# Attention and merge of a hybrid layer without GpSimd, and weight halves kept in DRAM

## The chip, the cores and the metric

The kernel runs on one core of a Trainium2 chip. It is timed as microseconds of device time for one launch; the time before is 2791.53 us, the median of three runs (2789.71 to 2792.70).

## The reference

One layer over 1024 tokens of width 1024 with a 256-token context: a layer norm, a projection, two branches (a bidirectional state-space scan with a gated output, and windowed attention of 8 query heads on 2 key heads with a sink in the softmax), a merge, a second norm and a mixture of experts (top 4 of 32). What the change touches is this part:

```
s_loc = where(|kpos - qpos| <= 128, q k^T, -1e30);  s_ctx = q kc^T
p = softmax([s_loc, s_ctx, sink]);  o_att = p_loc v + p_ctx vc
m = sig(g_ssm) * (z @ w_ssm_out) + sig(g_att) * (o_att @ w_att_out)
mix = m @ w_o
h = LN(alpha * h + gate1 * mix)
ffn = moe(modulate(h, shift2, scale2));  out = LN(alpha * h + gate2 * ffn)
```

All inputs and outputs are float32. The kernel keeps that precision by writing an operand as a rounded high half plus the rest, and by three matmuls (high by high, high by low, low by high) for each product.

## The kernel before

The program has three long parts. The first, up to about 545 us, holds the input norm, the projections and the scan. The second, from about 545 to 1130 us, runs attention, the branch outputs, the merge and the routing, woven into each other; the change lies here. The third, to the end, streams the weights of 32 experts.

In the second part `attention` (from L513) takes 8 blocks of 128 queries, each in two units, one for a key head. In a unit `scores` makes the scores of four query heads, two at a time: matmuls into PSUM, row maxima on DVE (L589 to L594), exponentials with row sums on ACT (L598, L600), the reciprocal of the sum on DVE (L604 to L606), and the normalisation of the probabilities P in place, on GpSimd (L608). `values` then transposes P on TensorE (L621), splits it into halves (ACT makes the high one, DVE the low one, L42 and L43) and multiplies by V.

A `Filler` puts pieces of other work between these steps: `glu` and `ssm_out`, beside which `residual` (L708) rescales the normed input row by row (a multiply and an add on GpSimd, L721 and L722), and then `merge` (L754). `merge` works on groups g of 256 tokens. `branches` needs two column pieces of w_att_out, `mix` four of w_o; each piece is 1 MB. `weights` (L793) keeps two pieces ready: `load_w` (L259) loads a raw piece, ACT writes its high half `whi`, and the low half `wlo` is made by GpSimd or by DVE in turn (`eng` in L795). The buffers `raw`, `whi` and `wlo` have two places each. So the first three groups take six pieces each; the last group takes two of w_att_out and two of w_o, and the two other pieces of w_o lie in buffers of their own, `wo` (L242), that are filled when attention has ended. `norm` (L850) makes the normed rows h and the modulated rows `xm`, whose last add is on GpSimd (L862). `residual2` (L1536) prepares the final sum for each of 8 token tiles: it loads a row block, multiplies it by a constant row on GpSimd (L1552), adds a small matmul on DVE (L1561), and stores it.

The order on each engine is set by a scheduler that places the instructions of the program when it is built, so a change of one engine shifts the order on all. All loads and stores of this part are issued from the one queue of SyncE (SP), in their order; an issue that has to wait holds up all behind it. From the last group's mixing on, the order of DVE, then also of TensorE and ACT, is the order of the code.

Of the kernel before, what the change touches and what calls it, by code (L numbers as in the profile page):

```python
# [8 lines left out]
F32 = mybir.dt.float32  # L9
F32R = mybir.dt.float32r  # L10
# [3 lines left out]
ACTF = mybir.ActivationFunctionType  # L14
ALU = mybir.AluOpType
# [7 lines left out]
KT = 8  # L23
# [5 lines left out]
ALPHA = 2.0 ** 0.25  # L29
# [52 lines left out]
def body(tc, a, o):  # L82
    nc = tc.nc
    K = Ctx()
    es = ExitStack()
    with es:
        cst = es.enter_context(tc.tile_pool(name="cst", bufs=1))
        dram = es.enter_context(tc.tile_pool(name="dram", bufs=1, space=DRAM))
        K.ident = cst.tile([128, 128], F32, name="ident")
        nc.sync.dma_start(out=K.ident, in_=a["ident"])  # L90
        K.cols = cst.tile([128, 68], F32, name="cols")
        nc.sync.dma_start(out=K.cols, in_=a["cols"])
        K.xhat_d = dram.tile([S, D], F32, name="xhat_d")
        K.rows_d = dram.tile([4, D], F32, name="rows_d")
        K.xm_d = dram.tile([S, D], F32, name="xm_d")
        K.acc_d = dram.tile([S + 128, D], F32, name="acc_d")
        K.kv_d = dram.tile([NCTX + S, 256], F32, name="kv_d")
        K.q_d = dram.tile([S, 512], F32, name="q_d")
        K.gate_d = dram.tile([16, 128, S], F32, name="gate_d")
        K.o_d = dram.tile([4, 128, S], F32, name="o_d")  # L100
        K.ssm_d = dram.tile([8, 128, S], F32, name="ssm_d")
        K.z_d = dram.tile([S, 512], F32, name="z_d")
        K.win_d = dram.tile([4, 128, 8 * 2 * 128], F32, name="win_d")
        K.wout_d = dram.tile([4, 128, 2 * 8 * 128], F32, name="wout_d")
        K.m_d = dram.tile([4, 128, 8 * 128], F32, name="m_d")
        K.tab_d = dram.tile([64, 34], F32, name="tab_d")
        K.tabe_d = dram.tile([64, 1], I32, name="tabe_d")
        K.cst = cst
        K.mask = cst.tile([128, 8, 2, 32], BF16, name="mask")
        K.gts = cst.tile([128, 8, 32], F32, name="gts")  # L110
        K.b_cols = a["b_cols"]
        pre(tc, a, K, es)
        moe(tc, a, K)
        finish(tc, a, o, K)
# [28 lines left out]
def pre(tc, a, K, top):  # L143
    nc = tc.nc
    es = ExitStack()
    with es:
# [88 lines left out]
        with ExitStack() as ws:  # L235
            wo = pool(ws, "wo")
            K.rk = pool(ws, "rk")
            rank_consts(tc, a, K, K.rk)
            K.ps = pool(ws, "lps", 2, space=PSUM)
            K.lp = pool(ws, "lgp", 1, space=PSUM)  # L240
            residual2_consts(tc, a, K, pool(ws, "res2"))
            K.wo = [load_w(tc, K, a["w_o"][:, c * 256:(c + 1) * 256], to=[wo.tile([128, KT, 256], F32R, name="wo%d%d" % (c, i)) for i in range(2)])  # L242
                    for c in range(2)]
            while not K.last:
                fl.emit()
            with tc.manual_schedule(engines={mybir.EngineType.DVE}):
                fl.drain()
                for r in K.todo:
                    next(r)
# [263 lines left out]
def attention(tc, a, K, es, fl):  # L513
    nc = tc.nc
# [19 lines left out]
    for g0, n in ((8, 2), (0, 4), (4, 4)):  # L534
        p = K.tp.tile([128, 512], F32, tag="tp", name="tp")
        for i in range(n):
            t = g0 + i
# [28 lines left out]
    def scores(n, kv, pr, Q):  # L566

        b0, b1 = max(0, n - 1), min(8, n + 2)
        nl = (b1 - b0) * 128
# [35 lines left out]
        nc.vector.tensor_tensor(su[:, 0], su[:, 0], su[:, 2], ALU.add)  # L605
        nc.vector.reciprocal(su[:, 0], su[:, 0])  # L606
        for i in range(2):
            nc.gpsimd.tensor_scalar(P[i][:, 0:nl + 256], P[i][:, 0:nl + 256], su[:, 0, i:i + 1], 1.0, ALU.mult, ALU.mult)  # L608
        return P

    def values(n, kv, P):
# [96 lines left out]
def residual(tc, a, K, es):  # L708

    nc = tc.nc  # L710
    pool = es.enter_context(tc.tile_pool(name="res", bufs=2, side="right"))
    for c in range(2):
        cs = slice(c * 512, (c + 1) * 512)
        gb = pool.tile([128, 2, 512], F32, tag="gb", bufs=1, name="gb")
        nc.sync.dma_start(out=gb, in_=a["ln_rows"][2:4, cs].unsqueeze(0).to_broadcast([128, 2, 512]))
        nc.gpsimd.tensor_scalar(gb, gb, ALPHA, 1.0, ALU.mult, ALU.mult)
        for t in range(8):
            x = pool.tile([128, 512], F32, tag="x", name="x")
            d = K.xhat_d[t * 128:(t + 1) * 128, cs]
            nc.sync.dma_start(out=x, in_=d)  # L720
            nc.gpsimd.tensor_tensor(x, x, gb[:, 0], ALU.mult)  # L721
            nc.gpsimd.tensor_tensor(x, x, gb[:, 1], ALU.add)  # L722
            nc.sync.dma_start(out=d, in_=x)
            yield

# [25 lines left out]
    return wn, out[:, 0], out[:, 1]  # L751


def merge(tc, a, K, es):  # L754

    nc = tc.nc
# [14 lines left out]
    def consts():  # L771
        nc.sync.dma_start(out=rb, in_=bc(K.rows_d[0:3], 3))
        v.tensor_scalar(G2, G2, 1.0, None, ALU.add)
        x0 = hp.tile([128, D], F32, tag="xm", name="x0")
        nc.sync.dma_start(out=x0, in_=a["ln_rows"][1:2, :].to_broadcast([128, D]))
        nc.gpsimd.tensor_tensor(x0, x0, G2, ALU.mult)
        nc.gpsimd.tensor_tensor(B2, B2, x0, ALU.add)
        x0 = hp.tile([128, D], F32, tag="xm", name="x0")
        nc.sync.dma_start(out=x0, in_=a["ln_rows"][0:1, :].to_broadcast([128, D]))
        nc.gpsimd.tensor_tensor(G2, G2, x0, ALU.mult)  # L780
        x0 = hp.tile([128, D], F32, tag="xm", name="x0")
        nc.gpsimd.memset(x0, 0.0)
        nc.sync.dma_start(out=K.acc_d[S:S + 128, :], in_=x0)
        nc.sync.dma_start(out=wr, in_=a["w_router"].rearrange("(k p) e -> p k e", p=128))
        nc.sync.dma_start(out=br, in_=a["b_router"].unsqueeze(0).to_broadcast([128, 32]))
        nc.sync.dma_start(out=e32, in_=a["route"][:, 384:416])

    sources = [s for g in range(4) for s in
               [(a["w_att_out"][:, c * 512:(c + 1) * 512], 512, 4) for c in range(2)] +
               [(a["w_o"][:, c * 256:(c + 1) * 256], 256, 8) for c in range(0 if g < 3 else 2, 4)]]  # L790
    ready = []

    def weights():  # L793
        while len(ready) < 2 and sources:
            ready.append(load_w(tc, K, *sources.pop(0), eng=nc.gpsimd if len(sources) % 2 else None))  # L795
        return ready.pop(0)

    def gates(g, c):
# [51 lines left out]
    def norm(g, h):  # L850
# [5 lines left out]
        for i in range(2):  # L856
            t = g * 2 + i
            v.tensor_scalar(h[i], h[i], mv[:, i, 0:1], r[:, i:i + 1], ALU.subtract, ALU.mult)
            nc.sync.dma_start(out=K.xhat_d[t * 128:(t + 1) * 128, :], in_=h[i])
            x = hp.tile([128, D], F32, tag="xm", name="xm")  # L860
            v.tensor_tensor(x, h[i], G2, ALU.mult)
            nc.gpsimd.tensor_tensor(x, x, B2, ALU.add)  # L862
            nc.sync.dma_start(out=K.xm_d[t * 128:(t + 1) * 128, :], in_=x)
            h[i] = x

# [670 lines left out]
def residual2(tc, K, t, h=None, eng=None, q=None):  # L1536
# [8 lines left out]
    for c in range(2):  # L1545
# [3 lines left out]
            nc.sync.dma_start(out=x, in_=K.xhat_d[t * 128:(t + 1) * 128, cs])  # L1549
        else:  # L1550
            x = h[:, cs]
        nc.gpsimd.tensor_tensor(x, x, K.ga[:, cs], ALU.mult)  # L1552
        xs.append(x)
    yield
    for c, x in enumerate(xs):
# [689 lines left out]
```

## Time and profile before

| what | value |
|---|---|
| median of three runs | 2791.53 us |
| the profiled execution | 2796.39 us |
| its span, first to last instruction | 2794.6 us |
| attention, branches, merge, routing | about 545 to 1130 us |
| busy over the span: PE, DVE, ACT, POOL | 90%, 80%, 52%, 17% |

The span is the time between the first and the last instruction of the profiled execution; 1.8 us lie around it. A busy share is an average over parts with different limits: the third part keeps TensorE nearly full, and the part that the change touches does not. PE is TensorE, PEld its weight loads, DVE VectorE, ACT ScalarE, POOL GpSimd, SP the queue that issues transfers.

### The profile page before, as it was taken

To read this page: it belongs to the slowest core of one execution; us is meant where nothing else is said; L and a number is where in the kernel's file an instruction comes from. 1 tells how busy PE (TensorE), PEld (TensorE's weight loads), DVE (VectorE), ACT (ScalarE), POOL (GpSimd) and SP (SyncE) were. 2 spreads that over 40 slices of the span, in tenths; PEclk is the share of its full clock that TensorE was granted. 3 is DMA by queue.
4 is the path that set the end of the run, shared out by engine and by line. 5 is a ranking of instruction groups with operands and counts; after the bars stand their busy time and mean duration, and the time that the engine had idled before them with its cause. 6 is when DMAs were issued, how large, how long until landed. Compare 5 with 4: busy or idle time off the path is not lost. (4 is left out here: it accounts for less than half of the span.)

```text
span 2794.6 us, 41588 instructions
## 1 busy us (share of the span) xinstructions
PE 2523.9 (90%) x14030; PEld 2123.3 (76%) x14030; DVE 2234.2 (80%) x4306; ACT 1465.9 (52%) x2352; POOL 465.0 (17%) x303
## 2 busy tenths in 40 slices
PE   6799999978887877699999999999999999999990
PEld 1698887767686767588888888889888887888770
DVE  9636796347788887788878888888988899899995
ACT  0623113656555422455656666666666666666661
POOL 3200000034333243210110110110111011101113
PEclk8799999979998877699999999999999999999995
DMA  7434623554454463678979978988998999899983
GB/s 252 155 125 157 202 87 116 161 172 136 163 169 139 146 195 102 209 244 266 290 226 284 295 242 283 292 273 272 303 294 262 305 301 300 275 305 302 311 280 144
DMA packets 409674, 631.11 MB, mean 226 GB/s; under 512 B 36497, under 2 KB 215569, under 8 KB 408497
## 3 DMA queue, kind: packets, MB, share of 16 engines
q1 hardware_dynamic: 397152, 584.37, 63.8%
q0 software_dynamic: 11872, 42.47, 6.5%
q8 instruction: 112, 1.84, 0.3%
q10 hardware_dynamic: 432, 1.57, 0.2%
q14 instruction: 106, 0.86, 0.1%
HBM read 551.76 MB, written 76.57 MB: 225 GB/s over the span
## 5 line engine op out<-in xcount | busy, mean ns | idle before, releaser
L1478 DVE TENSOR_TENSOR wl<-raw,wh 128x1024 fp32r<-128x1024 f32 x768 | 920.8, 1219 | 163.4 <-ACT wh L1476 162.3
L1476 ACT ACTIVATE wh<-raw 128x1024 fp32r<-128x1024 f32 x768 | 790.3, 1052 | 246.5 <-PE dn L1294 87.9
L1344 PE MATMUL uw<-x,wh 128*128 128x320 f32 (+5 forms) x1920 | 581.3, 366 | 0.2 <-issue 0.2
L1345 PE MATMUL uw<-x,wl 128*128 128x192 f32 (+4 forms) x1920 | 501.4, 261 | 0.0
L1344 PEld LDWEIGHTS uw<-x,wh 128*128 128x128 f32 x1920 | 364.3, 190 | 24.0 <-issue 0.3
L1345 PEld LDWEIGHTS uw<-x,wl 128*128 128x128 f32 x1920 | 369.6, 193 | 0.5
L1291 PE MATMUL dn<-wh,a 128*128 128x512 f32 (+4 forms) x752 | 298.7, 397 | 0.0
L1292 PE MATMUL dn<-wl,a 128*128 128x512 f32 (+4 forms) x752 | 293.6, 390 | 0.0
L1427 POOL DMA_INDIRECT acc_d<-y,wi x47 | 120.4, 2562 | 958.3 <-DVE y L1425 816.3
L1294 PE MATMUL dn<-wh,a 128*128 128x512 f32 (+3 forms) x608 | 238.5, 392 | 0.6 <-DVE a L1271 0.6
L1291 PE MATMUL up<-wh,x 128*128 128x512 f32 x544 | 221.8, 408 | 0.0
L1294 PE MATMUL up<-wh,x 128*128 128x512 f32 x544 | 213.0, 392 | 0.0
L1292 PE MATMUL up<-wl,x 128*128 128x512 f32 x544 | 212.3, 390 | 0.0
L1356 ACT ACTIVATE t<-uw,bias 128x160 f32<-128x160 f32 (+5 forms) x240 | 98.6, 419 | 134.5 <-PE uw L1345 131.6
L1291 PEld LDWEIGHTS dn<-wh,a 128*128 128x128 f32 (+4 forms) x752 | 135.7, 180 | 37.8 <-issue 4.1
L1292 PEld LDWEIGHTS dn<-wl,a 128*128 128x128 f32 (+4 forms) x752 | 135.8, 181 | 33.9
L608 POOL TENSOR_SCALAR P<-P,su 128x640 f32<-128x640 f32 (+1 forms) x64 | 55.1, 874 | 608.0 <-DVE su L606 543.9
L1294 PEld LDWEIGHTS dn<-wh,a 128*128 128x128 f32 (+3 forms) x608 | 112.8, 186 | 28.4 <-DVE a L1271 2.7
L42 ACT ACTIVATE whi<-raw 128x2048 fp32r<-128x2048 f32 x38 | 72.8, 1917 | 112.9 <-PE mm L53 72.5
L1240 POOL DMA_INDIRECT x<-xm_d,ri x47 | 53.3, 1135 | 463.3 <-DVE L L1202 304.0
L1291 PEld LDWEIGHTS up<-wh,x 128*128 128x128 f32 x544 | 102.3, 188 | 27.4 <-issue 8.4
L1294 PEld LDWEIGHTS up<-wh,x 128*128 128x128 f32 x544 | 102.1, 188 | 22.4
(532 smaller groups left out, 5349.2 us busy)
## 6 DMA issues: line engine op xcount, KB each, us to landing
raw<-w_gate_up SPq DMA_DIRECT2D x512, 512.0 KB
raw<-w_down SPq DMA_DIRECT2D x256, 512.0 KB
mw<-w_mod SPq DMA_DIRECT2D x64, 256.0 KB
raw<-w_o SPq DMA_DIRECT2D x16, 1024.0 KB
raw<-w_in SPq DMA_DIRECT2D x13, 1024.0 KB
raw<-w_mod SPq DMA_DIRECT2D x8, 1024.0 KB
gate_d<-gs SPq DMA_DIRECT2D x16, 512.0 KB
raw<-w_att_out SPq DMA_DIRECT2D x8, 1024.0 KB
```

The costliest lines, as they stand in the source:

```text
L42: nc.scalar.activation(out=hi, in_=src, func=ACTF.Copy)
L608: nc.gpsimd.tensor_scalar(P[i][:, 0:nl + 256], P[i][:, 0:nl + 256], su[:, 0, i:i + 1], 1.0, ALU.mult, ALU.mult)
L1240: nc.gpsimd.indirect_dma_start(out=x[0:nb], out_offset=None, in_=K.xm_d, bounds_check=S - 1, oob_is_err=True, in_offset=bass.IndirectOffse ...
L1291: nc.tensor.matmul(ps, lhsT=h, rhs=wh[:, k], start=st, stop=False)
L1292: nc.tensor.matmul(ps, lhsT=h, rhs=wl[:, k], start=False, stop=en and nb <= 64)
L1294: nc.tensor.matmul(ps, lhsT=X[:, k0 + k, lo:lo + nb], rhs=wh[:, k], start=False, stop=en)
L1344: nc.tensor.matmul(p[:, 0:2 * n], lhsT=wh[:, k, fs], rhs=self.x[:, k, 0:2 * n], start=k == 0, stop=False)
L1345: nc.tensor.matmul(p[:, 0:m], lhsT=wl[:, k, fs], rhs=self.x[:, k, 0:m], start=False, stop=k == KT - 1)
L1356: nc.scalar.activation(out=y[i], in_=self.uw[i][:, 1], func=ACTF.Identity, bias=self.bias[:, q * 8 + j0 + i:q * 8 + j0 + i + 1])
L1427: nc.gpsimd.indirect_dma_start(out=K.acc_d, out_offset=bass.IndirectOffsetOnAxis(ap=wi[0:nb], axis=0), in_=o[0:nb], in_offset=None, bounds ...
L1476: nc.scalar.activation(out=h, in_=r, func=ACTF.Copy)
L1478: nc.vector.tensor_tensor(l, r, h, ALU.subtract)
```

## The change

The normalisation of P goes from GpSimd to ACT (an activation that copies with a scale for each row). The rescaling in `residual`, the constants of `merge`, the last add of `norm`, and the multiply of `residual2` for the tiles whose rows are loaded go from GpSimd to DVE. The last group's tail (L924, L1565, and L1552 where h is given) and the constants of the experts stay on GpSimd. A new function `parts` replaces the loads of `merge`: the first time that a piece is needed, it is loaded and split as before (the low half always on DVE), and both halves are also stored to DRAM; every later time the two halves are read from there, 1 MB each, straight into `whi` and `wlo`.

```diff
@@ -106,6 +106,8 @@
         K.tab_d = dram.tile([64, 34], F32, name="tab_d")
         K.tabe_d = dram.tile([64, 1], I32, name="tabe_d")
         K.cst = cst
+        K.dram = dram
+        K.parts = {}
         K.mask = cst.tile([128, 8, 2, 32], BF16, name="mask")
         K.gts = cst.tile([128, 8, 32], F32, name="gts")
         K.b_cols = a["b_cols"]
@@ -239,8 +241,7 @@
             K.ps = pool(ws, "lps", 2, space=PSUM)
             K.lp = pool(ws, "lgp", 1, space=PSUM)
             residual2_consts(tc, a, K, pool(ws, "res2"))
-            K.wo = [load_w(tc, K, a["w_o"][:, c * 256:(c + 1) * 256], to=[wo.tile([128, KT, 256], F32R, name="wo%d%d" % (c, i)) for i in range(2)])
-                    for c in range(2)]
+            K.wo = [parts(tc, a, K, "o", c, [wo.tile([128, KT, 256], F32R, name="wo%d%d" % (c, i)) for i in range(2)]) for c in range(2)]
             while not K.last:
                 fl.emit()
             with tc.manual_schedule(engines={mybir.EngineType.DVE}):
@@ -605,7 +606,7 @@
         nc.vector.tensor_tensor(su[:, 0], su[:, 0], su[:, 2], ALU.add)
         nc.vector.reciprocal(su[:, 0], su[:, 0])
         for i in range(2):
-            nc.gpsimd.tensor_scalar(P[i][:, 0:nl + 256], P[i][:, 0:nl + 256], su[:, 0, i:i + 1], 1.0, ALU.mult, ALU.mult)
+            nc.scalar.activation(out=P[i][:, 0:nl + 256], in_=P[i][:, 0:nl + 256], func=ACTF.Copy, scale=su[:, 0, i:i + 1])
         return P
 
     def values(n, kv, P):
@@ -713,13 +714,13 @@
         cs = slice(c * 512, (c + 1) * 512)
         gb = pool.tile([128, 2, 512], F32, tag="gb", bufs=1, name="gb")
         nc.sync.dma_start(out=gb, in_=a["ln_rows"][2:4, cs].unsqueeze(0).to_broadcast([128, 2, 512]))
-        nc.gpsimd.tensor_scalar(gb, gb, ALPHA, 1.0, ALU.mult, ALU.mult)
+        nc.vector.tensor_scalar(gb, gb, ALPHA, None, ALU.mult)
         for t in range(8):
             x = pool.tile([128, 512], F32, tag="x", name="x")
             d = K.xhat_d[t * 128:(t + 1) * 128, cs]
             nc.sync.dma_start(out=x, in_=d)
-            nc.gpsimd.tensor_tensor(x, x, gb[:, 0], ALU.mult)
-            nc.gpsimd.tensor_tensor(x, x, gb[:, 1], ALU.add)
+            nc.vector.tensor_tensor(x, x, gb[:, 0], ALU.mult)
+            nc.vector.tensor_tensor(x, x, gb[:, 1], ALU.add)
             nc.sync.dma_start(out=d, in_=x)
             yield
 
@@ -751,6 +752,22 @@
     return wn, out[:, 0], out[:, 1]
 
 
+def parts(tc, a, K, m, c, to=None):
+
+    nc = tc.nc
+    kt, n = (4, 512) if m == "a" else (KT, 256)
+    hi, lo = to or (K.wp.tile([128, kt, n], F32R, tag=t, name=t) for t in ("whi", "wlo"))
+    if (m, c) in K.parts:
+        for t, d in zip((hi, lo), K.parts[m, c]):
+            nc.sync.dma_start(out=t.bitcast(F32), in_=d)
+    else:
+        load_w(tc, K, a["w_att_out" if m == "a" else "w_o"][:, c * n:(c + 1) * n], n, kt, to=(hi, lo))
+        K.parts[m, c] = [K.dram.tile([128, kt, n], F32, name="w%s%d%d" % (m, c, i)) for i in range(2)]
+        for t, d in zip((hi, lo), K.parts[m, c]):
+            nc.sync.dma_start(out=d, in_=t.bitcast(F32))
+    return hi, lo
+
+
 def merge(tc, a, K, es):
 
     nc = tc.nc
@@ -773,11 +790,11 @@
         v.tensor_scalar(G2, G2, 1.0, None, ALU.add)
         x0 = hp.tile([128, D], F32, tag="xm", name="x0")
         nc.sync.dma_start(out=x0, in_=a["ln_rows"][1:2, :].to_broadcast([128, D]))
-        nc.gpsimd.tensor_tensor(x0, x0, G2, ALU.mult)
-        nc.gpsimd.tensor_tensor(B2, B2, x0, ALU.add)
+        v.tensor_tensor(x0, x0, G2, ALU.mult)
+        v.tensor_tensor(B2, B2, x0, ALU.add)
         x0 = hp.tile([128, D], F32, tag="xm", name="x0")
         nc.sync.dma_start(out=x0, in_=a["ln_rows"][0:1, :].to_broadcast([128, D]))
-        nc.gpsimd.tensor_tensor(G2, G2, x0, ALU.mult)
+        v.tensor_tensor(G2, G2, x0, ALU.mult)
         x0 = hp.tile([128, D], F32, tag="xm", name="x0")
         nc.gpsimd.memset(x0, 0.0)
         nc.sync.dma_start(out=K.acc_d[S:S + 128, :], in_=x0)
@@ -785,14 +802,12 @@
         nc.sync.dma_start(out=br, in_=a["b_router"].unsqueeze(0).to_broadcast([128, 32]))
         nc.sync.dma_start(out=e32, in_=a["route"][:, 384:416])
 
-    sources = [s for g in range(4) for s in
-               [(a["w_att_out"][:, c * 512:(c + 1) * 512], 512, 4) for c in range(2)] +
-               [(a["w_o"][:, c * 256:(c + 1) * 256], 256, 8) for c in range(0 if g < 3 else 2, 4)]]
+    sources = [s for g in range(4) for s in [("a", c) for c in range(2)] + [("o", c) for c in range(0 if g < 3 else 2, 4)]]
     ready = []
 
     def weights():
         while len(ready) < 2 and sources:
-            ready.append(load_w(tc, K, *sources.pop(0), eng=nc.gpsimd if len(sources) % 2 else None))
+            ready.append(parts(tc, a, K, *sources.pop(0)))
         return ready.pop(0)
 
     def gates(g, c):
@@ -859,7 +874,7 @@
             nc.sync.dma_start(out=K.xhat_d[t * 128:(t + 1) * 128, :], in_=h[i])
             x = hp.tile([128, D], F32, tag="xm", name="xm")
             v.tensor_tensor(x, h[i], G2, ALU.mult)
-            nc.gpsimd.tensor_tensor(x, x, B2, ALU.add)
+            v.tensor_tensor(x, x, B2, ALU.add)
             nc.sync.dma_start(out=K.xm_d[t * 128:(t + 1) * 128, :], in_=x)
             h[i] = x
 
@@ -1549,7 +1564,7 @@
             nc.sync.dma_start(out=x, in_=K.xhat_d[t * 128:(t + 1) * 128, cs])
         else:
             x = h[:, cs]
-        nc.gpsimd.tensor_tensor(x, x, K.ga[:, cs], ALU.mult)
+        (nc.gpsimd if h is not None else v).tensor_tensor(x, x, K.ga[:, cs], ALU.mult)
         xs.append(x)
     yield
     for c, x in enumerate(xs):
```

Of the 24 pieces that the merge takes (6 + 6 + 6 + 4, and 2 in `wo`), 6 are made and stored, and 18 are read back.

The order around the change moves on three queues. First ACT, in two units of attention in the middle of the part. `sa` and `sb` are the scores, `su` the sums, `ph` the high half of the transposed P, `ot` part of an output. Before:

```order
L598 ACTIVATE P,su<-sa,nm 128x384
L600 ACTIVATE P,su<-sb,nm 128x256
L598 ACTIVATE P,su<-sa,nm 128x384
L600 ACTIVATE P,su<-sb,nm 128x256
L42 ACTIVATE ph<-tp 128x512 x2
L639 ACTIVATE ot<-pv 64x256
L640 ACTIVATE ot<-pv 64x256
L603 ACTIVATE su<-su 128x2
```

The same place of ACT with the change:

```order
L599 ACTIVATE P,su<-sa,nm 128x384
L601 ACTIVATE P,su<-sb,nm 128x256
L599 ACTIVATE P,su<-sa,nm 128x384
L601 ACTIVATE P,su<-sb,nm 128x256
L640 ACTIVATE ot<-pv 64x256
L641 ACTIVATE ot<-pv 64x256
L609 ACTIVATE P<-P,su 128x640 x2
L604 ACTIVATE su<-su 128x2
```

The normalisation L609 now stands on ACT, one or two instructions behind the exponentials; it needs the reciprocal that DVE makes from their sums.

Second SP, at the point where attention has ended. `wo` are the buffers of L242, `r` a piece of the residual, `x` the rows of `residual2`. Before:

```order
L1519 DMA br<-b_down 32x512 x2
L1520 DMA br<-ln_rows 64x512
L255 DMA raw<-w_o 128x8x256
L830 DMA r<-xhat_d 128x2x256
L255 DMA raw<-w_o 128x8x256
L830 DMA r<-xhat_d 128x2x256
L1549 DMA x<-xhat_d 128x512 x2
L255 DMA raw<-w_att_out 128x4x512
```

The same place of SP with the change:

```order
L1534 DMA br<-b_down 32x512 x2
L1535 DMA br<-ln_rows 64x512
L762 DMA wo_9072<-wo_6649 128x2048
L762 DMA wo_9073<-wo_6650 128x2048
L762 DMA wo_9076<-wo_6813 128x2048
L762 DMA wo_9077<-wo_6814 128x2048
L762 DMA whi<-wo_6950 128x2048
L762 DMA wlo<-wo_6951 128x2048
L845 DMA r<-xhat_d 128x2x256
L762 DMA whi<-wo_7086 128x2048
L762 DMA wlo<-wo_7087 128x2048
L845 DMA r<-xhat_d 128x2x256
```

Where two raw pieces of 1 MB stood ahead of the rows, eight halves of 1 MB stand there now; those for `whi` and `wlo` can be issued only when TensorE has finished with the buffer.

Third DVE, in the norm of the third group, after attention. Before:

```order
L72 SCALAR_TENSOR_TENSOR r_9471<-l1t,l1y 128x2
L858 TENSOR_SCALAR h<-h,mv_9470,r_9471 128x1024 x2
L861 TENSOR_TENSOR xm<-h,rb 128x1024 x2
L824 TENSOR_TENSOR gg<-gg,gs 128x256 x2
L823 TENSOR_TENSOR gg<-mm,gg 128x256
```

The same place of DVE with the change:

```order
L72 SCALAR_TENSOR_TENSOR r_9465<-l1t,l1y 128x2
L873 TENSOR_SCALAR h<-h,mv_9464,r_9465 128x1024 x2
L876 TENSOR_TENSOR xm<-h,rb 128x1024
L1567 TENSOR_TENSOR x<-x,ga 128x512 x2
L1576 TENSOR_TENSOR x<-pb,x 128x512 x2
L877 TENSOR_TENSOR xm<-xm,rb 128x1024
L876 TENSOR_TENSOR xm<-h,rb 128x1024
L1567 TENSOR_TENSOR x<-x,ga 128x512 x2
L877 TENSOR_TENSOR xm<-xm,rb 128x1024
```

The adds L877 and the multiplies L1567 have come in from GpSimd, and L1567 waits there for a load.

## Rows read from the trace of the kernel before

**Rows 1.** Windows: busy time of each engine, granted clock and DMA by stretch.

```profile
core 0: us, PE busy (x) PEld busy (x) DVE busy (x) ACT busy (x) POOL busy (x), PEclk, DMA share, GB/s
976.00:1130.00 154.00, 114.63 (x653) 97.70 (x651) 120.24 (x275) 42.25 (x82) 65.67 (x44) 0.76 0.45 147
976.80:982.40 5.60, 5.60 (x50) 5.60 (x49) 4.79 (x9) 3.59 (x3) 0.00 (x0) 1.00 0.95 287
1130.00:2794.60 1664.60, 1572.42 (x8573) 1328.21 (x8573) 1432.40 (x2642) 1017.35 (x1438) 198.56 (x104) 0.97 0.87 275
545.00:1130.00 585.00, 469.20 (x2833) 401.99 (x2833) 434.97 (x981) 277.60 (x626) 220.86 (x158) 0.87 0.45 149
```

**Rows 2.** Waits in 545:1130: who waited for whom, total, times, longest.

```profile
PE pv L633 <- DVE pl L43: 15.8, 7, 3.7
PE pv L632 <- DVE of L642: 11.9, 3, 7.0
PE sa L583 <- ACT P L598: 10.7, 8, 3.9
PE mm L51 <- DVE gg L823: 10.3, 3, 5.6
PE tp L933 <- POOL xm L862: 8.0, 1, 8.0
...
ACT su L603 <- DVE su L593: 40.3, 13, 7.3
...
SPq L255 <- POOL wlo L43: 49.8, 7, 12.6
```

**Rows 3.** Timeline of DVE and POOL, 884 us: start, length, instruction.

```profile
883.70 0.15 DVE L592 SCALAR_TENSOR_TENSOR nm<-nm,sink 128x2 f32<-128x2 f32 x1
...
884.06 4.52 POOL L43 TENSOR_TENSOR wlo<-raw,whi 128x2048 fp32r<-128x2048 f32 x1 [0.89 <-POOL P L608]
884.11 4.49 DVE L593 TENSOR_TENSOR su<-sink,nm 128x2 f32<-128x2 f32 x1
```

**Rows 4.** DVE by line and shape in 545:1130: count, busy us, mean ns.

```profile
L43 DVE TENSOR_TENSOR pl<-tp,ph 128x512 fp32r<-128x512 f32 x76 | 51.1, 683 | 5.7 <-ACT ph L42 5.2
L43 DVE TENSOR_TENSOR wlo<-raw,whi 128x2048 fp32r<-128x2048 f32 x14 | 33.0, 2357 | 11.5 <-ACT whi L42 11.5
...
L824 DVE TENSOR_TENSOR gg<-gg,gs 128x256 f32<-128x256 f32 x32 | 23.5, 751 | 3.1 <-DMA gs<-ssm_d 3.0
...
L593 DVE TENSOR_TENSOR su<-sink,nm 128x2 f32<-128x2 f32 x32 | 13.9, 433 | 0.8
L823 DVE TENSOR_TENSOR gg<-mm,gg 128x256 f32<-128x256 f32 x32 | 13.0, 415 | 3.2 <-PE mm L53 2.6 <-DMA gg<-gate_d 0.5
L861 DVE TENSOR_TENSOR xm<-h,rb 128x1024 f32<-128x1024 f32 x6 | 11.4, 1932 | 0.0
...
L604 DVE TENSOR_TENSOR su<-su 128x2 f32<-128x2 f32 x32 | 10.4, 326 | 10.9 <-ACT P L600 10.6
...
L605 DVE TENSOR_TENSOR su<-su 128x2 f32<-128x2 f32 x32 | 6.4, 201 | 1.5 <-ACT su L603 0.7
...
L606 DVE RECIPROCAL su<-su 128x2 f32<-128x2 f32 x32 | 5.1, 159 | 0.5
```

**Rows 5.** POOL by line and shape in 545:1130.

```profile
L43 POOL TENSOR_TENSOR wlo<-raw,whi 128x2048 fp32r<-128x2048 f32 x11 | 50.6, 4598 | 30.9 <-ACT whi L42 29.3 <-POOL P L608 1.6
L608 POOL TENSOR_SCALAR P<-P,su 128x640 f32<-128x640 f32 x48 | 43.5, 920 | 143.9 <-DVE su L606 94.6 <-PE sb L588 19.9 <-PE sa L586 11.8
L721 POOL TENSOR_TENSOR x<-x,gb 128x512 f32<-128x512 f32 x16 | 21.8, 1364 | 18.4 <-DMA x<-xhat_d 18.2
...
L1552 POOL TENSOR_TENSOR x<-x,ga 128x512 f32<-128x512 f32 x12 | 17.6, 1482 | 37.4 <-DMA x<-xhat_d 19.5 <-DVE pT L1116 15.3 <-DVE x L1561 2.6
L862 POOL TENSOR_TENSOR xm<-xm,rb 128x1024 f32<-128x1024 f32 x6 | 16.9, 2835 | 8.2 <-DVE xm L861 8.2
```

**Rows 6.** ACT by line and shape in 545:1130.

```profile
L42 ACT ACTIVATE whi<-raw 128x2048 fp32r<-128x2048 f32 x25 | 48.0, 1919 | 44.7 <-PE mm L53 23.3 <-PE mm L52 14.2 <-DVE h L843 7.2
...
L42 ACT ACTIVATE oh<-oraw 128x512 fp32r<-128x512 f32 x8 | 5.1, 634 | 2.2 <-DMA oraw<-o_d 2.2
...
L42 ACT ACTIVATE zth<-zt 128x1024 fp32r<-128x1024 f32 x4 | 4.2, 1060 | 0.1
```

## The prediction

> **What bounds the kernel now.** I read the windows first, by part, since the busy shares of the whole span mix parts with different limits. After 1130 us TensorE works 1572 of 1665 us at a granted clock of 0.97: that part is bound by TensorE, and the change leaves it alone [rows 1]. In the part that it touches, 545 to 1130 us, TensorE works 469 of 585 us at a clock of 0.87 and is idle for 116 us; DVE works 435 us, ACT 278, POOL 221, and the transfers take 45% [rows 1]. No engine is full. What bounds this part is the handing over between TensorE, DVE and ACT, step by step. So a busy time that is removed or added counts only where the next step waits for it.
>
> Then I read the waits of that part: TensorE waits mostly for DVE (the low half of the transposed P, the output factors, the gated branch) and for ACT's exponentials; once, for 8.0 us, for the last add of the norm on POOL; and ACT waits 40.3 us in all for the small sums of the softmax, L593, on DVE [rows 2]. L593 works on 128x2 elements. Why it is late stands in the timeline: it starts 0.05 us after a 4.52 us `wlo` of POOL and lasts 4.49 us, to that operation's end, while L592, of the same size and just before it, took 0.15 us [rows 3]. So a DVE instruction can be held for the length of a POOL instruction. This, and not POOL's 221 busy us as such, is what can be gained.
>
> **DVE held by POOL.** The shortest of the 128x2 forms, L606, takes 159 ns on average; L593 takes 433, so 32 x 0.274 = 8.8 us are lost there. Five others (of which L604 with 326 and L605 with 201 stand in the rows) lie between these; at their middle, 264, that is 5 x 32 x 0.105 = 16.8 us. L824 takes 751 ns where L823, of the same size, takes 415: 32 x 0.336 = 10.8 us. L861 takes 1932 where half a `wlo` (2357 for twice its elements) is 1179: 6 x 0.753 = 4.5 us [rows 4]. Together 41 us; with forms that have no twin to be measured by, I estimate 60. POOL keeps the constants of the experts and the tail, some 23 of its 221 us: the listed groups that move are 50.6 + 43.5 + 21.8 x 2 (L722 taken as L721) + 17.6 + 16.9 = 172 us [rows 5], the 16 norms of 128x512 are 12 more (0.92 x 512 / 640), and five larger constants, priced as L862, 14. So nine tenths of the hold go, some 53 of the 60 us. What share lies on the path? The held steps are mostly short steps of the softmax for which ACT, then TensorE, waits; I take 0.7: **-37 us** (from -53 to 0).
>
> **POOL's own steps on the path.** The 8.0 us wait of TensorE for L862 goes: the same add on DVE takes about 1.2 us, not 2.8. Loads wait 49.8 us for POOL's `wlo`, in seven waits [rows 2], mostly beside other work. The norm of P, 0.92 us each on POOL, is priced under ACT. I take **-12 us** (from -20 to 0).
>
> **DVE's new work.** L716, L721 and L722 of `residual`: 32 of 128x512 at 0.683, the price of the split `pl` of that shape, 21.9 us; and two larger constants, 2.4. The constants of `merge`: 3 x 1.18 = 3.5. L862: 6 x 1.18 = 7.1. L1552: 12 x 0.683 = 8.2. That is 43 us. Of 24 low halves POOL made 11 [rows 5] and DVE 13; now DVE makes 6: -7 x 2.357 = -16.5 [rows 4]. Net +26 us on 435 of 585. As DVE is the engine that TensorE waits for most, but has 150 us free, I charge a third: **+9 us** (from 0 to +26). It also gets a wait that it did not have: L1567 stands in DVE's order within the norm of the third group, and waits for a row block; POOL waited 19.5 us for these loads [rows 5]. Behind it on DVE stand the modulated rows and then the router. The blocks are issued well ahead, so I put nothing more on it than the 26.
>
> **ACT.** It loses 18 of its `whi`, 18 x 1.919 = -34.5 us, and gains 48 norms of 128x640, whose time lies between 634 (128x512) and 1060 ns (128x1024) [rows 6]; in proportion 740: +35.5, and 16 of 128x512, +10.1. Net +11 on 278 of 585 us. A pair of norms takes 1.5 us where POOL took 1.8. But POOL could wait for the reciprocal while ACT went on; now ACT waits, with the exponentials of the next unit and the splits of the transposed P queued behind. The wait is three short DVE steps, 0.5 us, 32 times: 15 us at most of this kind, against the 0.3 us gained on each pair: I take **+5 us** (from -5 to +46, which is all 64 norms on the path).
>
> **The weights.** Before: 24 loads of 1 MB. Now 6 loads, 12 stores, 36 loads: 54 MB. Beside the 149 GB/s of this part, which is 87 MB in 585 us, 30 MB more make 200 GB/s; a short stretch shows 287 GB/s at a share of 0.95 [rows 1], so full is 302. The volume fits. The order may not. A pair of halves takes 2 x 1.05 MB / 302 GB/s = 6.9 us at full rate; the 48 matmuls of a piece of w_o take 5.6 us at full clock [rows 1]. The buffers are two deep and a load can be issued only when TensorE has left the buffer, with the rows of `gates`, `residual` and the norm behind it on SP. Against this, a raw piece before took 3.5 us of loading, 1.9 of `whi` and 2.4 or 4.6 of `wlo` [rows 4 to 6], 8 to 10 us from issue to use, and TensorE's longest waits name other things [rows 2]; the pieces come spread over the part, since attention lies between. After attention, `wo` now needs 4 MB, with the next pair 6 MB, 20.8 us, before the last group's rows, in the window where TensorE is idle 39 of 154 us [rows 1]. I take **+3 us** (from -10 to +60).
>
> The Trainium skill, "DMA: Bandwidth & Descriptors" (section "Latency and other measured facts"), gives a fixed cost of about 2 us for a transfer, mostly the round trip of its receipt; nothing read here prices that apart. If each of the 18 pairs showed it once, the estimate by that page would be 36 us more and the gain gone; it speaks for the third rival below.
>
> **The clock.** Of the two levels, 1.2 and 2.4 GHz, 0.87 means that about a quarter of the time went by at the lower. Fewer gaps may raise it; from 0.87 to 0.97 on 469 us would give up to some 20 us on the path, since part of TensorE's time is hidden. I take 0.
>
> **Sum**: -37 - 12 + 9 + 5 + 3 = -32 us. The profiled execution took 2796.4 us, so 2764.4; the median of the runs is 4.9 us lower (0.17%), which gives **2760 us**. No difference can be told under 0.2%, 5.6 us.
>
> **Rivals.** *A, all of the hold was on the path.* -53 - 20 + 9 + 5 + 3 = -56, and the clock's -20: 2791.5 - 76 = 2716. For it: the held steps are those that ACT waits for, 40.3 us in one line alone [rows 2]. Against: while ACT waits, TensorE has the Filler's matmuls.
>
> *B, DVE becomes the bound.* Held DVE time was mostly hidden (share 0.3, -16), POOL's steps give -8, DVE's added work costs half of itself (+13), and +5 +3: -3, so 2789. For it: DVE ends most of TensorE's waits already [rows 2]. Against: even with all that is added DVE works less than before, 435 + 26 - 53. A change that does not do what it says would end here too: POOL keeps some 23 us, and if those lie where the holds hurt, little goes.
>
> *C, the read-back halves come late: slower.* One half's load, 3.5 us, stays bare for each of 18 pairs: +63 instead of +3, against -35 of the other terms: +28, 2820. It decides from 35 / 18 = 1.9 us bare on each pair. For it: 6.9 us of load against 5.6 us of use, and one queue in order. Against: the spacing of the pieces.
>
> **How the numbers follow.** Forecast, 2736 to 2780: 0.48; A 0.17; B 0.16; C 0.19. The range leaves out the lower third of A (0.06) and most of C (0.14): 2712 to 2806. Faster by over 0.2%: 0.48 + 0.17 and 0.05 of B, 0.70. Within: 0.08 of B and 0.01 of C, 0.09. Slower: 0.03 of B, 0.18 of C, 0.21.
>
> **What would show it.** The mean of L593 and its sisters near 160 ns and that of L824 near 415; POOL's busy time in this part near 23 us; ACT's wait for the sums short; the second part ending some 30 us before 1130, the third as long as before. C would show as TensorE waiting for the transfers of `parts` and SP waiting long for TensorE to leave `whi` and `wlo`; B as TensorE waiting longer for DVE with DVE's short forms at 160 ns. ACT's norm waiting for the reciprocal for more than 0.5 us a time would put the fourth term wrong. If the short forms stay above 250 ns, the main reason of the forecast is wrong.

## The result, and the profile after

| | before | changed |
|---|---|---|
| median of four runs | 2790.62 us | 2747.12 us |
| lowest to highest | 2785.92 to 2792.70 | 2746.35 to 2748.94 |
| span of the profiled execution | 2794.6 | 2746.8 |

The ratio is 0.9847, with a 95% interval of 0.9830 to 0.9864: about 43 us faster, in a range of 38 to 47. The forecast was 2760, in a range of 2712 to 2806.

The windows place it. Three stretches: from the first scores to the last product with V, from there to the first expert's matmuls, and the experts. The kernel before, with the columns of [rows 1]:

```profile
545.00:975.20 430.20, 353.77 (x2176) 303.49 (x2177) 314.32 (x704) 234.63 (x543) 155.19 (x114) 0.90 0.45 150
975.20:1149.50 174.30, 124.61 (x725) 106.50 (x723) 131.49 (x300) 47.85 (x91) 70.55 (x47) 0.73 0.49 161
1149.50:2794.60 1645.10, 1563.24 (x8508) 1320.21 (x8508) 1421.56 (x2620) 1012.48 (x1432) 193.68 (x100) 0.97 0.87 275
```

The changed kernel:

```profile
545.00:930.40 385.40, 339.61 (x2146) 291.42 (x2146) 287.81 (x740) 255.35 (x591) 2.19 (x2) 0.94 0.62 217
930.40:1105.70 175.30, 132.09 (x762) 111.12 (x760) 112.39 (x313) 33.97 (x86) 32.65 (x29) 0.73 0.64 229
1105.70:2746.80 1641.10, 1560.08 (x8508) 1317.60 (x8508) 1421.78 (x2620) 1011.93 (x1431) 192.41 (x100) 0.98 0.87 275
```

The spans of these two executions differ by 47.8 us, the medians by 43.5. Attention is 44.8 us shorter. The stretch behind it is 1.0 longer, the experts 4.0 shorter (no part of the change runs there). TensorE's idle time in the first two stretches, length less busy, falls from 76.4 + 49.7 to 45.8 + 43.2, by 37.1 us; its busy time falls by 6.7 for nearly the same number of matmuls (2901 and 2908), at a granted clock of 0.94 instead of 0.90 in attention. DVE loses 45.6 us of busy time although it took work over; ACT gains 6.8; POOL falls from 226 to 35.

DVE by line and shape in 545 to 1130 us of the changed kernel (count, busy us, mean ns). L594, L605, L606, L607, L838, L839 and L876 answer to L593, L604, L605, L606, L823, L824 and L861 of [rows 4]:

```profile
L43 DVE TENSOR_TENSOR pl<-tp,ph 128x512 fp32r<-128x512 f32 x76 | 51.6, 687 | 10.2 <-ACT ph L42 9.9
...
L838 DVE TENSOR_TENSOR gg<-mm,gg 128x256 f32<-128x256 f32 x32 | 13.2, 421 | 16.3 <-PE mm L53 16.1
...
L839 DVE TENSOR_TENSOR gg<-gg,gs 128x256 f32<-128x256 f32 x32 | 12.7, 420 | 1.7 <-DMA gs<-ssm_d 1.6
...
L876 DVE TENSOR_TENSOR xm<-h,rb 128x1024 f32<-128x1024 f32 x6 | 7.1, 1218 | 0.0
...
L594 DVE TENSOR_TENSOR su<-sink,nm 128x2 f32<-128x2 f32 x32 | 5.8, 182 | 0.4
...
L607 DVE RECIPROCAL su<-su 128x2 f32<-128x2 f32 x32 | 5.1, 160 | 0.5
L606 DVE TENSOR_TENSOR su<-su 128x2 f32<-128x2 f32 x32 | 5.1, 158 | 2.1 <-ACT su L604 1.1
...
L605 DVE TENSOR_TENSOR su<-su 128x2 f32<-128x2 f32 x32 | 5.0, 156 | 6.9 <-ACT P L601 6.4
```

Read the pair L838 and L839: before, the second took 751 ns for what the first does in 415; now they take 421 and 420. The first reads its product from PSUM and was never slow; nor was `pl`, 683 before and 687 now. The 128x2 steps shown are between 156 and 182.

The waits of TensorE up to 1105.7 us (total, times, longest), against [rows 2]:

```profile
PE mm L51 <- DVE gg L838: 7.8, 3, 6.4
...
PE pv L634 <- DVE pl L43: 6.2, 4, 3.7
PE pv L633 <- DVE of L643: 6.2, 2, 5.6
...
PE mm L53 <- DMA wlo<-wa: 3.4, 1, 3.4
```

The waits for `pl` fell from 15.8 to 6.2, for the output factors from 11.9 to 6.2, for the gated branch from 10.3 to 7.8; the 8.0 us for POOL's `xm` are gone. A new one is there, for a low half that is read back.

### The profile page after: what moved, and what is told of

The parts are those of the page before. It is cut to its first block, busy times and chain, and to the rows that moved or that the text cites. A ratio compares the mean times of both kernels' runs of the same rounds, so it can differ in the third digit from the quotient of the medians.

```text
span 2746.8 us, 41465 instructions
## 1 busy us (share of the span) xinstructions
PE 2513.2 (91%) x14030; PEld 2113.3 (77%) x14030; DVE 2190.4 (80%) x4354; ACT 1471.6 (54%) x2394; POOL 273.7 (10%) x173
## 5 line engine op out<-in xcount | busy, mean ns | idle before, releaser
L1307 PEld LDWEIGHTS up<-wl,x 128*128 128x128 f32 x544 | 102.4, 188 | 18.8
L51 PE MATMUL mm<-whi,uh 128*128 128x256 f32 x320 | 108.4, 339 | 4.4 <-DVE r L307 4.4
L52 PE MATMUL mm<-wlo,uh 128*128 128x256 f32 x320 | 107.7, 337 | 0.0
```

Source lines behind the costliest of these rows:

```text
L51: nc.tensor.matmul(out, lhsT=lsel(lh, k), rhs=rsel(rh, k), start=start and k == 0, stop=False)
L52: nc.tensor.matmul(out, lhsT=lsel(lh, k), rhs=rsel(rl, k), start=False, stop=False)
L1307: nc.tensor.matmul(ps, lhsT=h, rhs=wl[:, k], start=False, stop=en and nb <= 64)
```

## The experiments

Unless told otherwise a kernel is the changed one with the edit shown, in five rounds against the kernel before. The changed kernel, run once more beside the last group, gave 2751.42 (ratio 0.9856, 0.9836 to 0.9877), so differences of 4 us between medians of different groups tell nothing. Each expectation stands as it was written ahead of its run. What they call the hold theory is this: a DVE instruction beside certain GpSimd instructions ends only when these end, and the kernel pays for that time. An edit can also make the scheduler place the instructions anew. In the kernels with one part undone and in the one with one part alone, the traces show another order on TensorE, DVE and ACT than in the kernel that they are compared with, so their times are those of the edit together with its order. The two kernels with unused GpSimd work keep the changed kernel's order on these three engines, instruction by instruction, in this part of the program.

**One part undone: the normalisation of P.**

```
-nc.scalar.activation(out=P[i][...], in_=P[i][...], func=ACTF.Copy, scale=su[:, 0, i:i + 1])
+nc.gpsimd.tensor_scalar(P[i][...], P[i][...], su[:, 0, i:i + 1], 1.0, ALU.mult, ALU.mult)
```

> The changed kernel with one part undone: the 64 normalisations of P run on GpSimd again (some 56 us of GpSimd work). If the gain came from DVE no longer being held by GpSimd, the 128x2 steps of DVE are held again for part of their time and the time rises by 8 to 18 us against the changed kernel (2747). If GpSimd mattered only as a slow producer, the rise is under 5 us, since ACT takes 0.82 us for what GpSimd did in 0.92. If ACT's new work is what limits attention now, the time falls by up to 10 us.

Measured: 2754.91, ratio 0.9869 (0.9849 to 0.9889), 3 to 8 us above the changed kernel, not told apart from it for sure. This is under the 8 to 18 us of the hold theory. GpSimd's 64 operations (970 ns each for the larger) held DVE little: in 545 to 1130 us of this kernel

```profile
L839 DVE TENSOR_TENSOR gg<-gg,gs 128x256 f32<-128x256 f32 x32 | 13.9, 454 | 2.9 <-DMA gs<-ssm_d 2.7
...
L594 DVE TENSOR_TENSOR su<-sink,nm 128x2 f32<-128x2 f32 x32 | 5.3, 167 | 1.1
```

So 59 us of GpSimd work cost 3 to 8 us at most, and L594 stayed at 167 ns. It does hold DVE where the two meet; two of the 128x2 steps (start, length):

```profile
791.72 0.38 DVE L592 TENSOR_TENSOR nm<-mx 128x2 f32<-128x2 f32 x1
792.13 0.74 DVE L593 SCALAR_TENSOR_TENSOR nm<-nm,sink 128x2 f32<-128x2 f32 x1
```

and the pair of normalisations beside them:

```profile
791.29 1.58 POOL L609 TENSOR_SCALAR P<-P,su 128x640 f32<-128x640 f32 x2 [9.89 <-DVE su L607]
```

L593 ends at 792.87, as the pair does, after 0.74 us instead of some 0.16. Taken together, the step to ACT and the GpSimd work that it removes are a small gain at most, and not a loss.

**One part undone: the row arithmetic** (L717, L722, L723, the constants of the merge, L877, L1567):

```
-v.tensor_tensor(x, x, B2, ALU.add)
+nc.gpsimd.tensor_tensor(x, x, B2, ALU.add)
...
```

> The changed kernel with the row arithmetic (residual, constants of the merge, last add of the norm, multiply of residual2) on GpSimd again, some 95 us of GpSimd work. Hold theory: 15 to 30 us slower than the changed kernel, with the 128x2 steps of DVE and the gated branch longer again, and TensorE waiting again for the modulated rows. Rival, that DVE's added 43 us are paid on the path: 5 to 15 us faster than the changed kernel.

Measured: 2767.99, ratio 0.9921 (0.9901 to 0.9942): 17 to 21 us slower than the changed kernel, within what the hold theory said; DVE's busy time in 545 to 1130 us is 13 us less than in the changed kernel and the kernel is slower. L594 takes 233 ns, and TensorE waits 4.3 us for `xm` from POOL again. The gated branch is not longer, other than expected: L839 takes 418 ns.

**One part undone: the copies in DRAM,** the low halves on DVE; and the same with the low halves in turn, as before:

```
-            ready.append(parts(tc, a, K, *sources.pop(0)))
+            ready.append(load_w(tc, K, *piece(a, *sources.pop(0))))
```

```
+            m, c = sources.pop(0)
+            ready.append(load_w(tc, K, *piece(a, m, c), eng=nc.gpsimd if len(sources) % 2 else None))
```

In both, the two pieces in `wo` are loaded raw as well.

> The changed kernel without the DRAM copies: each of the 24 weight pieces is loaded raw and split anew, the high half by ACT and the low half always by DVE (18 more of each: 35 us of ACT, 42 us of DVE). GpSimd's low halves stay away. Hold theory: the DRAM copies are not what gained; within -8 to +12 us of the changed kernel, since the waits for late read-back halves after attention (some 15 us on TensorE's chain) go and DVE and ACT work come back. Rival, that ready halves are the main gain: 20 to 40 us slower.

> The changed kernel with the weight pieces as in the kernel before: loaded raw each time, the low half by GpSimd and DVE in turn (11 of GpSimd's 128x2048 subtractions of 4.6 us, 50 us in all). Hold theory: 10 to 25 us slower than the changed kernel, and slower than the kernel with all low halves on DVE although that gives DVE 26 us more work. Rival, that DVE's busy time decides: faster than the kernel with all low halves on DVE.

Measured: 2747.47, ratio 0.9839 (0.9820 to 0.9858), without copies: the same as with them. With the low halves in turn 2781.36, ratio 0.9963 (0.9947 to 0.9979). The edits of the two differ in nothing but which engine makes 11 low halves: 34 us for 57 us of GpSimd's work, where 59 us of the normalisation cost 3 to 8. That is more than the 10 to 25 that were expected. It need not be the hold alone: the order of the engines differs too, and SP's loads wait 44.5 us for GpSimd's low halves, though TensorE itself waits for them only 1.3 us. DVE with the halves in turn:

```profile
L845 DVE TENSOR_TENSOR gg<-gg,gs 128x256 f32<-128x256 f32 x32 | 17.0, 549 | 1.2 <-DMA gs<-ssm_d 1.1
L605 DVE TENSOR_TENSOR su<-su 128x2 f32<-128x2 f32 x32 | 9.9, 310 | 9.1 <-ACT P L601 8.5
```

and TensorE's wait in this kernel:

```profile
PE pv L634 <- DVE pl L43: 25.8, 10, 5.8
```

With the low halves on DVE this wait is 5.4 us. `pl` itself is not held (its median is 683 ns here too); as I read it, it comes late because held steps stand ahead of it on DVE. Where the copies' cost and gain lie, the windows of the kernel without them show:

```profile
546.70:941.30 394.60, 345.94 (x2183) 295.82 (x2183) 308.75 (x754) 273.81 (x603) 0.95 (x1) 0.94 0.49 163
941.30:1101.90 160.60, 121.84 (x725) 104.45 (x723) 127.04 (x317) 47.83 (x92) 33.02 (x30) 0.73 0.53 173
```

Attention takes 9.2 us more without copies, the stretch behind it 14.7 less; part of both is 37 matmuls that are done in the one stretch or the other.

**One part alone.** The kernel before with one edit:

```
-            ready.append(load_w(tc, K, *sources.pop(0), eng=nc.gpsimd if len(sources) % 2 else None))
+            ready.append(load_w(tc, K, *sources.pop(0)))
```

> The kernel before with one edit: all low halves of the merge's weights are made by DVE, none by GpSimd (11 more of 2.36 us on DVE, 26 us). Everything else stays, the normalisation and the row arithmetic on GpSimd too. Hold theory, with the cost growing with the length of the single GpSimd instruction: 20 to 38 us faster than the kernel before, although DVE gets more work. Rival, that each part of the change counts by its GpSimd time: 50 of about 198 us, 9 to 13 us faster. Rival, that DVE's busy time decides: 5 to 15 us slower.

Measured: 2764.55, ratio 0.9912 (0.9892 to 0.9932), 25 us faster. This one line, with the new order that comes with it, is over half of the whole gain, and DVE has 11 low halves more. The kernel with all but this (halves in turn, above) gained 10; the two together, without copies, 43. The 8 us by which 43 is more than 25 and 10 are not clear of the noise, as each of the three is known to some 5 us.

**GpSimd work that nobody uses.** The spare buffer is that of the raw pieces, which stands empty once the six have been made:

```
+            if len(K.parts) == 6 and len(sources) % 3:
+                x = K.wp.tile([128, KT, 256], F32, tag="raw", name="idle").rearrange("p k n -> p (k n)")
+                nc.gpsimd.memset(x, 0.0)
+                nc.gpsimd.tensor_tensor(x, x, x, ALU.add)
```

> The changed kernel with GpSimd work that nobody uses: beside 12 of the 18 read-back pieces GpSimd fills a spare 128x2048 buffer with zeros and adds it to itself, about 4.6 us an add. Hold theory: DVE's short steps that fall beside these adds last until the add ends, and the time rises by 8 to 25 us against the changed kernel (2747), with no instruction waiting for GpSimd's result. Rival, that GpSimd cost only where its results were awaited: within 3 us.

Measured: 2783.08, ratio 0.9983 (0.9971 to 0.9995): 32 to 36 us slower, more than the 8 to 25 that the hold theory expected, for 60 us of GpSimd work, all done within 781 to 848 us. No instruction on TensorE, DVE or SP waits for it. POOL at 780 us of this kernel (start, length):

```profile
782.71 3.60 POOL L814 TENSOR_TENSOR idle<-idle 128x2048 f32<-128x2048 f32 x1
...
788.25 3.60 POOL L814 TENSOR_TENSOR idle<-idle 128x2048 f32<-128x2048 f32 x1
```

and DVE beside it:

```profile
782.14 0.15 DVE L594 TENSOR_TENSOR su<-sink,nm 128x2 f32<-128x2 f32 x1
...
782.87 3.46 DVE L595 TENSOR_SCALAR nm<-nm 128x2 f32<-128x2 f32 x1
...
788.92 2.95 DVE L605 TENSOR_TENSOR su<-su 128x2 f32<-128x2 f32 x1
791.90 0.16 DVE L606 TENSOR_TENSOR su<-su 128x2 f32<-128x2 f32 x1
```

L595 ends at 786.33, the add at 786.31; L605 ends at 791.87, the add at 791.85. Steps of the same size (L594 and L606) take 0.15 us a moment before and after. This shows the hold by itself: work without a reader on GpSimd, in an unchanged order of the other engines, 32 to 36 us on the kernel.

**The same work in short pieces,** sixteen of 128x128 for each:

> As the kernel with unused GpSimd work, but each zeroing and each add of 128x2048 cut into 16 of 128x128: the same elements in 16 times as many instructions. Hold theory by length: DVE is held for at most one short piece at a time, and the cost against the changed kernel falls from 36 us to under 15. Rival, that GpSimd takes a fixed share of DVE's time while it works, however it is cut: 30 us or more, since the pieces together last longer.

Measured: 2777.61, ratio 0.9952 (0.9935 to 0.9968), 26 to 30 us slower than the changed kernel. The time is near the rival's 30, but DVE is hardly held (over the whole part L594 182 ns, L605 154). SP's queue shows another cause, with its echo on DVE:

```profile
SPq L1598 <- POOL idle L814: 31.0, 1, 31.0
```

```profile
DVE gg L843 <- DMA gg<-gate_d: 26.2, 1, 26.2
```

A load of the experts' constants uses the same buffer, stands early in SP's queue, and had to wait for the unused work; the gates were queued behind it. The wait lasts until 876 us; the stretch before DVE stands still for it can be compared. L594 runs twice in each unit of attention; the windows go from the start of the 19th to that of the 25th, three units with the same work for TensorE, DVE and ACT, in the changed kernel, with long pieces and with short pieces (columns as in [rows 1]):

```profile
783.00:846.80 63.80, 57.28 (x390) 49.98 (x389) 53.02 (x144) 40.96 (x102) 0.27 (x1) 0.92 0.80 275
782.10:882.40 100.30, 68.25 (x391) 57.66 (x390) 89.35 (x143) 42.11 (x104) 59.16 (x23) 0.76 0.51 176
787.70:853.90 66.20, 56.93 (x390) 48.87 (x388) 59.27 (x143) 41.35 (x102) 66.08 (x226) 0.92 0.72 256
```

The second run of the changed kernel takes 62.1 us for them. With 59 us of unused work in long pieces the three units take 36 to 38 us more, and DVE's busy time is 36 us longer; with 66 us of it in short pieces they take 2 to 4 us more and DVE works 6 longer. From the 25th L594 to the 26th, where DVE waits for the gates, it is 35.1 us instead of 7.0. So the run's time is that of the late load, and this stretch shows what was asked: of the same operations in the same order, long ones cost, short ones hardly.

**The late halves after attention.** One more pair of buffers (every third read-back pair in the buffers of the raw pieces, three kept ready):

```
+        tags = ("raw", "raw") if K.turn == 0 else tags
```

> The changed kernel with room for one more read-back piece: every third pair goes into the two buffers of the raw pieces, which stand empty then, and three pieces are kept ready. If the waits of TensorE for read-back halves after attention (some 15 us) come from the two-deep buffers, the time falls by 5 to 12 us. If they come from the volume of transfers after attention (6 MB before the third group can go on), it falls by less than 4 us.

Measured: 2753.03, ratio 0.9876 (0.9857 to 0.9896). 2 to 6 us above the changed kernel: more room for the pieces gained nothing. Then the two pieces of `wo` loaded raw, 2 MB for 4:

```
-            K.wo = [parts(tc, a, K, "o", c, [...]) for c in range(2)]
+            K.wo = [load_w(tc, K, *piece(a, "o", c), to=[...]) for c in range(2)]
```

> The changed kernel with the two pieces of w_o in buffers of their own loaded raw and split (2 MB instead of 4 MB) at the end of attention. Volume theory: the waits for halves after attention shrink by the 2 MB, 7 us at 302 GB/s, and the time falls by 4 to 9 us. Buffer theory: no change within 3 us.

Measured: 2747.01, ratio 0.9856 (0.9836 to 0.9876): no change from 2747.12, and 4 us under the second median; the 4 to 9 us are not shown. And all pieces raw from the end of attention on:

```
-    if (m, c) in K.parts:
+    if (m, c) in K.parts and K.late is None:
```

> The changed kernel that reads halves back only while attention runs and loads and splits raw pieces from its end on. The stretch of attention should stay at the changed kernel's 385 us and that after it go to the 160 us of the kernel without copies: 10 to 15 us faster than the changed kernel. Rival, that DVE and ACT, which then split again, slow the end as much as the late halves did: within 4 us.

> The kernel that reads halves back only while attention runs, once more, beside the changed kernel on the same chip: 3 to 12 us faster than it if its shorter end is real; within 2 us if the four microseconds between their medians were the chip's.

> The changed kernel once more, as the measure for the three others: 2747 us, within 4 us.

Measured: 2743.46, ratio 0.9844 (0.9824 to 0.9863), and again 2743.02, ratio 0.9825 (0.9808 to 0.9843), against 2747.12 and 2751.42 of the changed kernel. Both medians are lower, by 4 and 8 us, and the stretch after attention is shorter in both profiles; in the second one

```profile
545.80:930.10 384.30, 339.71 (x2146) 291.99 (x2146) 286.76 (x740) 255.91 (x592) 0.95 (x1) 0.94 0.64 221
930.10:1100.00 169.90, 129.98 (x761) 110.32 (x759) 128.86 (x321) 48.93 (x94) 34.45 (x30) 0.74 0.54 178
```

5.4 us less than 175.3, at the same attention. As a gain, 4 and 8 us are less than the 10 to 15 that were expected; the first is within the rival's 4 and the second is not. In the pair that ran beside each other each of the five runs (2737.24 to 2746.32) is below each of the four of the changed kernel (2747.03 to 2753.07); the intervals of the ratios just overlap, so I call it likely and not settled. It is the fastest of the kernels that were run.

## Why the prediction was right

The forecast was 32 us faster, and 43 was measured (38 to 47). Its direction and its main mechanism held; the sizes of its terms held only in part, and some no run shows singly.

**The hold** was the main term and is shown by the unused work; the low halves alone agree. DVE's means came out as forecast (near 160 and 420 ns). What DVE lost: the seven 128x2 groups 28 us (64.6 to 36.3), L824 and L861 15, and forms that had no twin to be measured by (`ml`, `zl`, `zsig`, `h`, `ol`) 20, together 63 us where I had 53. At the share of 0.7 that is 7 of the 11 us by which the sum was short. The share itself can't be measured here: in the three units with the unused work in long pieces all 36 us of it came through to the time, so 0.7 is not a constant of the kernel. POOL kept 34.8 us up to the first expert where 23 were forecast; the forecast's part ended at 1130 us, ahead of some of the tail.

**How I shared it out was wrong.** I took off nine tenths of the hold since nine tenths of GpSimd's busy time went. It goes more by the length of the single instruction: the unused work shows it at one kind and one order. The parts of the change agree, though their order differs too: the low halves (5.15 us each, 57 us in all) cost 34 us, the row arithmetic (mostly 1.4 to 2.7 us each, some 90 us) 17 to 21, the normalisation (0.97 us or less, 59 us) 3 to 8. I take it that a short one is often over before DVE comes to a form that it holds, and a long one is not. The normalisation differs from the low halves in kind too (one tensor and a value for each row, against two tensors), but it holds as well where it meets a step. How much of the differences between the parts is length, kind or order is not settled.

**The 40.3 us of ACT waiting for L593** [rows 2] were misread. I took them as a sign of the hold and said they would be short. In the changed kernel:

```profile
ACT su L604 <- DVE su L594: 42.0, 14, 7.3
```

They are still there, with the step itself at 182 ns instead of 433. This wait is the way from the scores over the row maxima, whoever holds DVE. So the sign "ACT's wait for the sums short" did not come, though the mechanism held. What shrank were TensorE's waits for `pl` and the output factors. A wait names the last step before it, not the step that is too long.

**DVE's new work, +9**, is not separable, but rival B is out: DVE's busy time fell by 45.6 us, and moving the row arithmetic or the low halves to DVE gained each time, with the order that came with it.

**ACT, +5**: the busy time was near (+6.8 us for +11). The price can't be read by itself: undoing the step brings 59 us of GpSimd work back with it, and both together made the kernel no faster. ACT by line in 545 to 1130 us of the changed kernel (740 and 634 ns were taken):

```profile
L609 ACT ACTIVATE P<-P,su 128x640 f32<-128x640 f32 x48 | 37.1, 822 | 8.5 <-DVE su L607 8.0 <-DVE r L72 0.5
...
L609 ACT ACTIVATE P<-P,su 128x512 f32<-128x512 f32 x16 | 10.6, 712 | 0.4 <-DVE su L607 0.4
```

It waited for the reciprocal 8.4 us in all; 15 was my bound. These are 12 waits of 0.7 us on average, above the 0.5 that I had named as a sign against this term, but only for 12 of the 32 pairs.

**The weights, +3**: the copies, taken together with the splits that they save ACT and DVE, changed nothing, 2747.1 with them and 2747.5 without. How late the halves come, which the term was meant for, was not run by itself. Rival C is out: for the 18 pairs it wanted 1.9 us bare on each, and TensorE waits for read-back halves 5.2 us in all, after attention. While attention spaces the pieces out, SP waits for TensorE to leave `whi` and `wlo`, and TensorE never for a half; up to 930 us:

```profile
SPq L762 <- PE mm L53: 25.4, 7, 12.3
```

**The clock, 0**, rose from 0.90 to 0.94 in attention, in step with TensorE's busy time, which fell by 6.7 us over the two stretches for nearly the same number of matmuls. So this term was not nothing. The experts' stretch, -4.0 us in the profiled pair, has no part in the change; it took between 1641 and 1647 us in the kernels that were run.

## What to carry to other kernels

Look for DVE instructions that take several times the shortest of their kind, and see in the timeline whether they end with a GpSimd instruction: then GpSimd's time is not free, though nobody waits for its results. Take the longest operations off GpSimd first; here that gained even where DVE, the busier engine, took them over. Work that is kept in memory and read back was no worse, perhaps better, in the stretch where other work spaces the loads out, and likely worse in the one where little stands between them, so look at the two apart. When a run with an added load or buffer comes out slow, read the queue that issues the loads before you take its time for an answer.

## What the runs showed of the hardware that was not expected

Which DVE forms are held can be read from the means before and after. Those that read PSUM kept theirs (`pl` 683 and 687 ns, L823 and L838 415 and 421), as did those on one tensor such as the reciprocal of 128x2 (159 and 160). Those on two tensors in SBUF fell (L824 to L839, 751 to 420), and so did a tensor with a constant (L594 282 to 166 as L595). The Trainium skill, "SBUF — State Buffer" (section "Who interferes with whom"), states such a division: a DVE instruction with two SBUF inputs contends for a shared port pair with a GpSimd instruction that reads SBUF, not with one that only writes; one in a two-port mode, as a tensor with a scalar can be, contends with GpSimd; and the loser waits for the whole instruction. The traces agree, with holds that end within 0.02 us of GpSimd's add. They agree on the part that only writes, too. Among the unused work are zeroings, which only write; beside two of them

```profile
815.75 3.55 POOL L813 MEMSET idle<- 128x2048 f32 x2
```

L594, on two tensors, is not held, and L595, a tensor with a constant, is, to their end at 819.30:

```profile
816.99 0.11 DVE L594 TENSOR_TENSOR su<-sink,nm 128x2 f32<-128x2 f32 x1
817.13 2.20 DVE L595 TENSOR_SCALAR nm<-nm 128x2 f32<-128x2 f32 x1
```

That GpSimd work without any reader can cost over half of its own length in the kernel's time, 32 to 36 us for 60, was more than I expected; in short pieces it cost 2 to 4 us for 66, in the stretch that can be compared.
